# First MLP product of a hybrid decoder block by pairs of column tiles: seven block products in place of eight

## The chip, the cores and the metric

The kernel runs on one core of one Trainium2 chip. The metric is the device time of one execution in microseconds (us), less is better. The core has TensorE (PE in the profile; its weight loads stand apart as PEld), VectorE (DVE), ScalarE (ACT), GpSimd (POOL) and SyncE (SP). The engines run beside each other. Each does its own instructions in the order in which they were written into its queue, and where it needs another engine's result it waits on a semaphore. SyncE's queue issues nearly all the transfers of this kernel.

## The reference, cut to what matters

One layer, 512 positions, width 2048, float32: a mixing sub-layer, then an MLP with a squared ReLU. The change is in the MLP.

```python
# x: (1, 512, 2048); w_ff1: (2048, 8192); w_ff2: (8192, 2048)
x = x + gate1 * (merged @ w_out)
h2 = modulate(rms_norm(x, norm2_g), shift2, scale2)   # rms_norm * (1 + scale2) + shift2
ff = square(relu(h2 @ w_ff1)) @ w_ff2
x = x + gate2 * ff
```

## The kernel before

Everything is held transposed: 128 channels on the partitions, the 512 positions along the free dimension. `h2` is 16 tiles of 128x512 (one for each 128 of the 2048 channels), the hidden layer 64 such tiles, the result `x1` 16.

**Three matmuls for one.** The products are of float32 accuracy from operands of a shorter type (`fp32r`). `split` (L243) makes two tiles of one: ScalarE writes the rounded high part (`hi`), VectorE the remainder (`lo`). `mm3` (L247) issues three matmuls into one PSUM bank: `whi` by `x_hi`, `whi` by `x_lo`, `wlo` by `x_hi`. Each matmul has a weight load of its own.

**Items.** The matmul work is a list of items of 512 weight columns (four weight blocks of 128x128, twelve matmuls). `step` (L334) takes the next one: `pump_loads` issues the transfers of weights for which a buffer `raw` is free (three of 1024 columns), `pump_splits` writes the splits of the items up to two further on into the queues of ScalarE and VectorE (`whi`, `wlo`, four buffers each), then `emit` issues the matmuls and `post` what follows at the end of a tile. So the order on every engine is the order of these calls. A split two items ahead stands in the queue before the work of the present item's `post`.

**Norm stage.** The last tile of the output projection and the first four hidden tiles (`first_emit`, L702) are interleaved by halves of 256 positions with the making of `h2` (`scale_h2`, `shift_h2`, L638 to L650): here, and nowhere else in the products, matmuls stream 256 columns.

**MLP.** The hidden tiles go in eight groups of eight. `add_tile` (L280) of a hidden tile has four items, 48 matmuls. `ff1_post` (L761) applies ReLU and square on ScalarE and splits the result. When a group's eight hidden tiles are there, the second product runs over its share of K: for each of 16 output tiles two items (24 matmuls), then `ff2_post` (L772) adds the product times the gate to `x1[n]` on VectorE. PSUM has eight banks: three of the pool `acc` (every tile's sums) and five of `mx`.

**Memory.** SBUF is one pool `act` with tags: `A` (32 tiles: `h`, later `h2`), `O` (25 tiles: mixing stages, then the hidden tiles), `C`, `T`, `L` and so on.

Of the kernel before, what the change touches and what calls it, by code (L numbers as in the profile page):

```python
# [31 lines left out]
FIRST = ("ident", "adaT")  # L32
SKEW = (1, 3)
# [54 lines left out]
def tile_block(ctx, tc, xT, cT, wada1, wada2, badaT, g1T, g2T, wg0, win, wbat, wbhg, wout, wfg, wff1, wff2,  # L88
               lbT, hggT, qgT, kgT, sinks, table, ident_d, mask_d, onehot_d, neg_d, outT):
# [10 lines left out]
    dram = ctx.enter_context(tc.tile_pool(name="dram", bufs=1, space=bass.MemoryType.DRAM))  # L100

# [59 lines left out]
    def take(tag, shape=None, dt=F32, name=None):  # L161
        pl.live[tag] = pl.live.get(tag, 0) + 1
        return act.tile(shape or [P, T], dt, tag=tag, bufs=BUFS[tag], name=nm(name or tag))

# [51 lines left out]
    ones = fst.tile([P, P], F32, name="ones")  # L216
# [6 lines left out]
    bones = fst.tile([P, P], F32, name="bones")  # L223
# [53 lines left out]
    def add_item(ld, c0, w, emit, pre=None, post=None):  # L277
        items.append((ld, c0, w, emit, pre, post))
# [32 lines left out]
    ahead_of = {}  # L311
    state = {"load": 0, "split": 0, "item": 0}
# [12 lines left out]
    def pump_splits(upto):  # L325
        while state["split"] < min(upto + 1, len(items)):
            ld, c0, w, *_ = items[state["split"]]
            hi = act.tile([P, w], F32R, tag="whi", bufs=BUFS["whi"], name=nm("whi"))
            lo = act.tile([P, w], F32R, tag="wlo", bufs=BUFS["wlo"], name=nm("wlo"))
            split(raws[ld][:, c0:c0 + w], hi, lo)  # L330
            wts[state["split"]] = (hi, lo)
            state["split"] += 1

    def step(ahead=AHEAD, drive=True):  # L334
# [5 lines left out]
        _, _, _, emit, pre, post = items[i]  # L340
# [3 lines left out]
        if post:  # L344
            post()
        if drive:
# [13 lines left out]
    def ada_acc():  # L360
        return act.tile([P, T], F32, tag="aa", bufs=1, name=nm("aa"))

    def ada_rest():
# [4 lines left out]
        def fetch(n):  # L368
            while len(raw) < min(n + BUFS["ada"], 256):
                t = act.tile([P, T], F32, tag="ada", bufs=BUFS["ada"], name=nm("ada"))  # L370
# [213 lines left out]
    def out_post(n):  # L584
        def post(ps):
# [12 lines left out]
            if n == KT - 2:  # L598
                pl.until(lambda: not pl.gens)
                stt(G2, adaT[:, 64:80], 1.0, g2_sb, ALU.add, ALU.mult)  # L600
# [10 lines left out]
    h2 = []  # L611
    kept = []
# [25 lines left out]
    def scale_h2(kt, c=slice(0, T)):  # L638
        if kt == len(h2):
            h2.append((take("A", dt=F32R), take("A", dt=F32R)))  # L640
        t = sqs[kt] = take("T")
        stt(t[:, c], x1[kt][:, c], G2[:, kt:kt + 1], sqs["r"][:, c], ALU.mult, ALU.mult)

    def shift_h2(kt, c=slice(0, T)):
        hi, lo = part(h2[kt], c)
        t = sqs.pop(kt)
# [3 lines left out]
        drop("T")  # L650
# [108 lines left out]
    a_t = {g: [] for g in range(8)}  # L759

    def ff1_post(g):  # L761
        def post(ps):
            r = take("T")
# [622 lines left out]
```

## Time and profile before

| | us |
|---|---|
| median of 3 runs (lowest, highest) | 2766.82 (2766.62, 2767.34) |
| the profiled execution | 2767.79 |
| its span in the trace | 2766.0 |
| TensorE busy in the span | 2743.4 |
| weight loads busy | 2225.9 |
| VectorE busy | 1306.0 |
| ScalarE busy | 932.0 |
| mean granted TensorE clock | 0.999 of 2.4 GHz |

Busy time of TensorE counts overlapping matmuls once, and the ends of matmuls are modelled, so the distance from start to start says more than a duration. The trace gives every instruction with its start, its shape (partitions x columns), and where an engine stood idle the instruction whose end released it. Between span and device time lie 1.8 us, which the change doesn't touch.

### The profile page before, as it was taken

Reading aid. Unit: us, or ns where it says so; the run is one execution under the profiler, and the core shown is the slowest. Engines: PE = TensorE matmul, PEld = TensorE weight load, DVE = VectorE, ACT = ScalarE, POOL = GpSimd, SP = SyncE. Lnnn points to the kernel's source line nnn. Section 1 sums busy time; section 2 is a strip of 40 time slices with the busy share of each in tenths; the row PEclk is TensorE's granted clock in tenths of the full one; section 3 lists DMA queues with packets and bytes.
Section 4 is the critical chain, followed back from the end, with each engine's and each line's share of the span. In section 5 each row is a group of like instructions: output and inputs, shape, how many; then the busy total and the mean of one; then the engine's idle time right before and its main releaser. Section 6 shows DMA issues by size and latency. Waiting matters only on the chain.

```text
span 2766.0 us, 33013 instructions
## 1 busy us (share of the span) xinstructions
PE 2743.4 (99%) x12630; PEld 2225.9 (80%) x12630; DVE 1306.0 (47%) x2574; ACT 932.0 (34%) x1686; POOL 14.5 (1%) x28
## 2 busy tenths in 40 slices
PE   8999999999999999999999999999999999999999
PEld 4777777888888888888888888888888888888887
DVE  4778787655544555565443333332332333323323
ACT  4244455544222322232342332422323223232231
POOL 1000000000000000000000000000000000000000
PEclk9999999999999999999999999999999999999999
DMA  8852322444555555555322222222222322222233
GB/s 322 291 182 93 126 88 73 145 137 138 191 194 191 188 181 184 181 183 186 100 98 101 91 100 99 92 99 99 99 96 96 99 98 93 99 99 92 99 111 111
DMA packets 133790, 369.50 MB, mean 134 GB/s; under 512 B 15168, under 2 KB 15296, under 8 KB 133632
## 3 DMA queue, kind: packets, MB, share of 16 engines
q1 hardware_dynamic: 132480, 364.96, 38.9%
q0 software_dynamic: 1152, 2.43, 0.3%
q8 instruction: 99, 1.62, 0.2%
q14 instruction: 59, 0.48, 0.1%
HBM read 363.11 MB, written 4.23 MB: 133 GB/s over the span
## 4 chain that ended last, share of the span: by engine, by line
PE 97%; DVE 2%; ACT 1%; DMA 0%; issue 0%; SPq 0%; ACTq 0%
PE acc L153 87%; PE mx L153 9%; PE mx L157 1%; DMA C<-xT 0%; DVE wlo L116 0%; ACT T L149 0%; DVE T L120 0%; DVE L L120 0%; DVE T L116 0%; ACT A L149 0%; ACT whi L149 0%; DVE s L1002 0%; DVE C L120 0%; DVE A L120 0%; DVE C L127 0%
## 5 line engine op out<-in xcount | busy, mean ns | idle before, releaser
L153 PE MATMUL acc<-A,whi 128*128 128x512 f32 (+1 forms) x4608 | 1421.7, 390 | 2.4 <-ACT A L149 1.9
L153 PEld LDWEIGHTS acc<-A,whi 128*128 128x128 f32 x4608 | 857.8, 188 | 191.8 <-issue 8.9
L153 PE MATMUL acc<-A,wlo 128*128 128x512 f32 (+1 forms) x2304 | 894.5, 388 | 1.4 <-DVE wlo L116 1.4
L149 ACT ACTIVATE whi<-raw 128x512 fp32r<-128x512 f32 x944 | 569.8, 626 | 918.2 <-PE acc L153 882.6
L116 DVE TENSOR_TENSOR wlo<-raw,whi 128x512 fp32r<-128x512 f32 x944 | 625.9, 686 | 354.9 <-ACT whi L149 354.3
L153 PE MATMUL acc<-O,whi 128*128 128x512 f32 x2560 | 787.9, 389 | 0.0
L153 PEld LDWEIGHTS acc<-O,whi 128*128 128x128 f32 x2560 | 480.5, 188 | 99.7
L153 PEld LDWEIGHTS acc<-A,wlo 128*128 128x128 f32 x2304 | 432.9, 188 | 91.8 <-DVE wlo L116 2.2
L153 PE MATMUL acc<-O,wlo 128*128 128x512 f32 x1280 | 497.9, 389 | 0.0
L120 DVE SCALAR_TENSOR_TENSOR C<-acc,adaT,C 128x512 f32<-128x512 f32 x128 | 96.1, 751 | 432.5 <-PE acc L153 432.5
L153 PEld LDWEIGHTS acc<-O,wlo 128*128 128x128 f32 x1280 | 240.2, 188 | 50.0
L116 DVE TENSOR_TENSOR O<-T,O 128x512 fp32r<-128x512 f32 x64 | 44.4, 693 | 381.7 <-ACT O L149 381.7
L149 ACT ACTIVATE T<-acc 128x512 f32<-128x512 f32 x92 | 55.0, 598 | 460.3 <-PE acc L153 460.3
L387 DVE SCALAR_TENSOR_TENSOR ada<-ada,aa 128x512 f32<-128x512 f32 x256 | 175.6, 687 | 38.3 <-DMA ada<-wada 33.9
L153 PE MATMUL mx<-A,whi 128*128 128x512 f32 (+1 forms) x448 | 134.4, 383 | 3.6 <-ACT A L149 2.5
L153 PEld LDWEIGHTS mx<-A,whi 128*128 128x128 f32 x448 | 81.9, 189 | 25.7 <-issue 5.0
L153 PE MATMUL mx<-A,wlo 128*128 128x512 f32 (+1 forms) x224 | 84.1, 375 | 0.0
L149 ACT ACTIVATE T<-T 128x512 f32<-128x512 f32 (+1 forms) x102 | 62.6, 621 | 6.0 <-DVE T L116 3.4
L149 ACT ACTIVATE T<-C 128x512 f32<-128x512 f32 (+1 forms) x33 | 20.1, 616 | 94.1 <-DVE C L120 90.0
L153 PEld LDWEIGHTS mx<-A,wlo 128*128 128x128 f32 x224 | 42.3, 189 | 8.1
L116 DVE TENSOR_TENSOR O<-mx,O 128x512 f32<-128x512 f32 x56 | 37.9, 688 | 17.1 <-PE mx L153 16.2
L149 ACT ACTIVATE C<-acc 128x512 f32<-128x512 f32 x26 | 15.5, 598 | 86.5 <-PE acc L153 86.5
(155 smaller groups left out, 980.6 us busy)
## 6 DMA issues: line engine op xcount, KB each, us to landing
raw<-wff SPq DMA_DIRECT2D x248, 512.0 KB, 3.3
raw<-win SPq DMA_DIRECT2D x128, 512.0 KB, 3.7
ada<-wada SPq DMA_DIRECT2D x256, 256.0 KB, 4.0
O<-wada SPq DMA_DIRECT2D x128, 256.0 KB, 5.1
raw<-wout SPq DMA_DIRECT2D x32, 512.0 KB, 3.7
raw<-wg SPq DMA_DIRECT2D x24, 512.0 KB, 4.5
raw<-wbat SPq DMA_DIRECT2D x16, 512.0 KB, 3.4
raw<-wbhg SPq DMA_DIRECT2D x16, 512.0 KB, 3.7
```

Source lines behind the costliest of these rows:

```text
L116: nc.vector.tensor_tensor(out=out, in0=in0, in1=in1, op=op)
L120: nc.vector.scalar_tensor_tensor(out=out, in0=in0, scalar=scalar, in1=in1, op0=op0, op1=op1)
L149: nc.scalar.activation(out=out, in_=in_, func=func, **kw)
L153: PE.matmul(out, lhsT=lhsT, rhs=rhs, start=start, stop=stop)
L157: PE.transpose(out=out, in_=in_, identity=ident)
L387: nc.vector.scalar_tensor_tensor(out=t, in0=t, scalar=1.0, in1=cb, op0=ALU.mult, op1=ALU.mult, accum_out=adaq[:, i, q:q + 1])
```

## The change

Two hidden tiles are computed together. The weights of a pair, over two neighbouring channel tiles `e` and `o` of `h2`, are a 2x2 arrangement of 128x128 blocks; `h2` over these two channel tiles and the two halves `a`, `b` of the positions is a 2x2 arrangement of 128x256 blocks. The product of two 2x2 arrangements is done with seven block products instead of eight (Winograd's form of Strassen's scheme): sums of blocks are formed on both sides before, and sums of the products after. Each block product is still three matmuls, now of 256 columns.

- `t_sums`, `t_split`, `t_last` make the four sums of `h2` blocks for each of the eight channel pairs, once, and split them. They overwrite the second half of each even tile of `h2`. `scale_h2` keeps its 16 tiles for it (tag `B`).
- `split_seven` prepares one unit (two channel pairs) of a weight pair: three blocks and four sums of blocks for each, as `hi` and `lo` of 1792 columns (tag `wt`, four buffers, that replaces `whi` and `wlo`).
- `seven_pair` issues four units of 84 matmuls into four banks; `sums1` to `sums3` put the seven products together on VectorE, and ReLU and square follow on ScalarE.
- Hidden tiles 0 to 3 are made as before. Tiles 4 and 5 (`wfp`) are made whole, since the sums are not there yet; tiles 6 to 63 are 29 pairs.
- The second product goes in 16 groups of four hidden tiles (`ff2_group`): 12 matmuls for each output tile, then `ff2_post`.
- A list `todo` holds the sums, the splits of hidden tiles and the `h2` sums; one entry is run at the end of each item. In the last group the first four output tiles take the two hidden tiles that are there first, and the other two after.
- Memory: tags `O` and `L` and the conditioning loads move to a pool `mid` that is closed at the end of the output projection; a pool `mlp` with 32 tiles `B` (sums of `h2`, hidden tiles) takes its place. GpSimd's DMA scratch is set to 1024 bytes.

```diff
-BUFS = {"A": 32, "O": 25, "C": 16, "T": 6, "L": 5, "ada": 3, "raw": 3, "whi": 4, "wlo": 4}
+BUFS = {"A": 32, "O": 25, "C": 16, "T": 6, "L": 5, "ada": 3, "raw": 3, "wt": 4, "B": 32, "S": 1}
+WT = 7 * 2 * P
...
     def pump_splits(upto):
         while state["split"] < min(upto + 1, len(items)):
-            ld, c0, w, *_ = items[state["split"]]
-            hi = act.tile([P, w], F32R, tag="whi", bufs=BUFS["whi"], name=nm("whi"))
-            lo = act.tile([P, w], F32R, tag="wlo", bufs=BUFS["wlo"], name=nm("wlo"))
-            split(raws[ld][:, c0:c0 + w], hi, lo)
-            wts[state["split"]] = (hi, lo)
+            ld, c0, w, *_, prep = items[state["split"]]
+            wts[state["split"]] = prep(raws[ld][:, c0:c0 + w])
...
         if post:
             post()
+        if todo:
+            todo.pop(0)()
...
+    def t_sums(j):
+        a, b = HALF
+        e, o = bare[2 * j], bare[2 * j + 1]
+        sb = adaT[:, 49 + 2 * j:50 + 2 * j]
+        x, y = take("T"), take("T")
+        tt(x[:, a], e[:, b], e[:, a], ALU.subtract)
+        stt(x[:, b], x[:, a], sb, o[:, b], ALU.subtract, ALU.subtract)
+        stt(y[:, a], e[:, b], sd[:, j:j + 1], o[:, b], ALU.add, ALU.subtract)
+        tt(y[:, b], o[:, b], o[:, a], ALU.subtract)
+        tt(y[:, b], y[:, b], x[:, a], ALU.subtract)
...
+    def t_split(j):
...
+        hi, lo = take("B", dt=F32R), take("B", dt=F32R)
+        split(y, hi, lo)
...
+        split(x[:, b], z[:, 0, :], z[:, 1, :])
...
+    def t_last(j):
...
+        hi, lo = part(h2[2 * j], b)
+        split(tb[j][0][:, a], hi, lo)
...
+    def split_seven(raw):
+        hi, lo = wt(), wt()
+        s = take("S", [P, 8 * P])
...
+        tt(v(s[:, 0:2 * c]), v(raw[:, 0:2 * c]), raw[:, 3 * c:4 * c][:, None, :].to_broadcast([P, 2, c]), ALU.add)
+        sact(hi[:, 0:3 * c], raw[:, 0:3 * c], AF.Copy)
+        tt(s[:, 2 * c:3 * c], s[:, 0:c], raw[:, c:2 * c], ALU.add)
+        sact(hi[:, 3 * c:5 * c], s[:, 0:2 * c], AF.Copy)
+        tt(s[:, 3 * c:4 * c], s[:, 2 * c:3 * c], raw[:, 2 * c:3 * c], ALU.add)
+        sact(hi[:, 5 * c:7 * c], s[:, 2 * c:4 * c], AF.Copy)
+        tt(lo[:, 0:3 * c], raw[:, 0:3 * c], hi[:, 0:3 * c].bitcast(F32), ALU.subtract)
+        tt(lo[:, 3 * c:7 * c], s, hi[:, 3 * c:7 * c].bitcast(F32), ALU.subtract)
...
+    def seven_pair(p, now):
...
+                for kp in range(2):
...
+                    for ps, c, w, x in ((b0, a, B11, part(e, a)), (b1, a, B12, part(o, a)), (b1, b, S2, t2),
+                                        (b2, a, S3, t3), (b2, b, S1, t1), (b3, a, B22, t4), (b3, b, S4, part(o, b))):
+                        w += kp * P
+                        mm3(ps[:, c], hi[:, w:w + P], lo[:, w:w + P], x, first and c is a,
+                            last and (c is b or ps is b0))
...
+        def sums1():
...
+            sact(e2[:, 0, :], b0[:, HALF[0]], AF.Copy)
+            tt(e1, b1.rearrange("p (n c) -> p n c", n=2), e2[:, 0:1, :].to_broadcast([P, 2, T // 2]), ALU.add)
...
+        def sums2():
...
+            tt(e2, e1[:, 1:2, :].to_broadcast([P, 2, T // 2]), b2, ALU.subtract)
+            tt(e1[:, 1, :], e2[:, 0, :], b2[:, 1, :], ALU.subtract)
...
+        def sums3():
...
+            tt(e2, e2, b3, ALU.add)
...
+            sact(r0[:, a], e1[:, 0, :], AF.Relu)
+            sact(r0[:, b], e2[:, 1, :], AF.Relu)
+            sact(r0, r0, AF.Square)
...
+            if now:
+                todo.extend([lambda: hidden(r0, g), lambda: hidden(r1, g)])
+            else:
+                waiting.extend([r0, r1])
...
+        for u in range(4):
+            ahead_of[len(items)] = 1 if u < 3 else 2
+            add_item(add_load(wst[p - 3, u], 1024), 0, 1024, unit(u), None, post if u == 3 else None, split_seven)
...
-    for g in range(8):
-        for i in range(8):
-            n = 8 * g + i
-            if n >= GF:
-                add_tile(halves(wff1, n - GF), ready(h2), ff1_post(g))
-        a0 = len(items)
-        for n in range(KT):
-            add_tile([wff2[g, n]], ready(a_t[g]), ff2_post(g, n))
...
+    for i in range(2):
+        add_tile(halves(wfp, i), ready(h2), tiles45(i), (lambda: todo.extend(
+            [shift_diff, lambda: t_sums(0), lambda: t_split(0), lambda: t_sums(1), lambda: t_split(1)])) if i == 1 else None)
+    ff2_group(0)
+    for g in range(1, NG):
+        seven_pair(2 * g + 1, True)
+        if g < NG - 1:
+            seven_pair(2 * g + 2, False)
+        ff2_group(g)
```

What this does to the queues is shown at three places. First TensorE in the middle of the MLP. Before, a hidden tile is one bank (`acc`) with rows of 512 columns:

```order
L153 MATMUL acc_13116<-A_11500,whi_13071 128x512
L153 MATMUL acc_13116<-A_11501,whi_13071 128x512
L153 MATMUL acc_13116<-A_11500,wlo_13072 128x512
L153 MATMUL acc_13116<-A_11536,whi_13071 128x512
L153 MATMUL acc_13116<-A_11537,whi_13071 128x512
L153 MATMUL acc_13116<-A_11536,wlo_13072 128x512
```

After, the first unit of the pair of tiles 10 and 11 (`A`: `h2`, `B`: sums of `h2`, `wt`: weights and their sums):

```order
L163 MATMUL mx_12916<-A_11076,wt_12858 128x256
L163 MATMUL mx_12916<-A_11077,wt_12858 128x256
L163 MATMUL mx_12916<-A_11076,wt_12859 128x256
L163 MATMUL mx_12917<-A_11111,wt_12858 128x256
L163 MATMUL mx_12917<-A_11112,wt_12858 128x256
L163 MATMUL mx_12917<-A_11111,wt_12859 128x256
L163 MATMUL mx_12917<-B_11687,wt_12858 128x256 x2
L163 MATMUL mx_12917<-B_11687,wt_12859 128x256
L163 MATMUL mx_12918<-B_11683,wt_12858 128x256
L163 MATMUL mx_12918<-B_11684,wt_12858 128x256
L163 MATMUL mx_12918<-B_11683,wt_12859 128x256
```

The rows are half as wide, there are seven triples for each channel pair, and they go round four banks.

Second VectorE in the second product of the first group. Before, two remainders of weights and one sum into `x1` for each output tile:

```order
L120 SCALAR_TENSOR_TENSOR C_10393<-acc_12384,adaT,C_10393 128x512
L116 TENSOR_TENSOR wlo_12417<-raw_12329,whi_12416 128x512
L116 TENSOR_TENSOR wlo_12434<-raw_12329,whi_12433 128x512
L120 SCALAR_TENSOR_TENSOR C_10481<-acc_12420,adaT,C_10481 128x512
L116 TENSOR_TENSOR wlo_12453<-raw_12365,whi_12452 128x512
L116 TENSOR_TENSOR wlo_12470<-raw_12365,whi_12469 128x512
L120 SCALAR_TENSOR_TENSOR C_10569<-acc_12456,adaT,C_10569 128x512
```

After, over two output tiles (`sd`: differences of the shifts; `T` to `B`, `T` to `A`: sums of `h2`):

```order
L126 TENSOR_TENSOR wt_11918<-raw_11784,wt_11918 128x512
L130 SCALAR_TENSOR_TENSOR C_10514<-acc_11921,adaT,C_10514 128x512
L126 TENSOR_TENSOR A_11310<-T_11904,A_11309 128x256
L126 TENSOR_TENSOR wt_11937<-raw_11784,wt_11937 128x512
L130 SCALAR_TENSOR_TENSOR C_10598<-acc_11942,adaT,C_10598 128x512
L126 TENSOR_TENSOR T_11956<-B_11355 128x256
L130 SCALAR_TENSOR_TENSOR T_11956<-T_11956,adaT,B_11376 128x256
L130 SCALAR_TENSOR_TENSOR T_11957<-B_11355,sd,B_11376 128x256
L126 TENSOR_TENSOR T_11957<-B_11376 128x256
L126 TENSOR_TENSOR T_11957<-T_11957,T_11956 128x256
L126 TENSOR_TENSOR B_11964<-T_11957,B_11963 128x512
L126 TENSOR_TENSOR B_11967<-T_11956,B_11967 128x256
```

Between the weights' remainders now stand a sum into `x1` for every item and the eight instructions of one channel pair's `h2` sums.

Third TensorE at the end of the last first product. Before, the second product follows with the first of eight hidden tiles, whole:

```order
L153 MATMUL acc_20524<-A_11904,whi_20537 128x512
L153 MATMUL acc_20524<-A_11905,whi_20537 128x512
L153 MATMUL acc_20524<-A_11904,wlo_20538 128x512
L153 MATMUL acc_20600<-O_20060,whi_20555 128x512
L153 MATMUL acc_20600<-O_20061,whi_20555 128x512
L153 MATMUL acc_20600<-O_20060,wlo_20556 128x512
L153 MATMUL acc_20600<-O_20136,whi_20555 128x512
L153 MATMUL acc_20600<-O_20137,whi_20555 128x512
L153 MATMUL acc_20600<-O_20136,wlo_20556 128x512
```

After, behind the last unit of the last pair (`mx_23085`), each output tile begins with two hidden tiles, and goes to the next:

```order
L163 MATMUL mx_23085<-A_11462,wt_23187 128x256
L163 MATMUL mx_23085<-A_11463,wt_23187 128x256
L163 MATMUL mx_23085<-A_11462,wt_23188 128x256
L163 MATMUL acc_23304<-B_23065,wt_23242 128x512
L163 MATMUL acc_23304<-B_23066,wt_23242 128x512
L163 MATMUL acc_23304<-B_23065,wt_23242 128x512
L163 MATMUL acc_23304<-B_23128,wt_23242 128x512
L163 MATMUL acc_23304<-B_23129,wt_23242 128x512
L163 MATMUL acc_23304<-B_23128,wt_23242 128x512
L163 MATMUL acc_23330<-B_23065,wt_23245 128x512
L163 MATMUL acc_23330<-B_23066,wt_23245 128x512
L163 MATMUL acc_23330<-B_23065,wt_23245 128x512
```

The other two hidden tiles of each output tile come after the fourth.

## Rows read from the trace of the kernel before

**Rows 1.** The page's parts 1 and 4: busy time by engine; chain that ended last.

```profile
PE 2743.4 (99%) x12630; PEld 2225.9 (80%) x12630; DVE 1306.0 (47%) x2574; ACT 932.0 (34%) x1686; POOL 14.5 (1%) x28
PE 97%; DVE 2%; ACT 1%; DMA 0%; issue 0%; SPq 0%; ACTq 0%
```

**Rows 2.** Stretches: window; busy us (instructions) by engine; granted clock; DMA share; GB/s.

```profile
1359.14:1362.38 3.24, 3.24 (x29) 3.24 (x28) 2.02 (x5) 1.41 (x4) 0.00 (x0) 1.00 0.00 0
1371.67:1378.50 6.83, 6.83 (x59) 6.83 (x57) 4.48 (x11) 3.08 (x6) 0.00 (x0) 1.00 0.13 53
1413.20:2762.40 1349.20, 1349.13 (x5953) 1116.79 (x5951) 442.69 (x686) 408.85 (x683) 0.00 (x0) 1.00 0.29 98
```

**Rows 3.** Chain of work in order of time, its last long piece: start, us, what.

```profile
1413.22 1349.13 PE acc L153 x5952
```

**Rows 4.** Timeline, TensorE: start, us, operation x count; 256 columns, then 512 columns.

```profile
1373.85 0.40 PE L153 MATMUL mx<-A,whi 128*128 128x256 f32 x2
1374.09 0.28 PE L153 MATMUL mx<-A,wlo 128*128 128x256 f32 x1
1374.21 0.42 PE L153 MATMUL mx<-A,whi 128*128 128x256 f32 x2
1374.48 0.28 PE L153 MATMUL mx<-A,wlo 128*128 128x256 f32 x1
...
2390.89 0.62 PE L153 MATMUL acc<-O,whi 128*128 128x512 f32 x2
2391.57 0.62 PE L153 MATMUL acc<-O,whi 128*128 128x512 f32 x2
```

**Rows 5.** Timeline, weight loads of the same two kinds of stretch.

```profile
1361.06 0.19 PEld L153 LDWEIGHTS acc<-A,wlo 128*128 128x128 f32 x1
1361.18 0.31 PEld L153 LDWEIGHTS acc<-A,whi 128*128 128x128 f32 x2
...
2391.35 0.41 PEld L153 LDWEIGHTS acc<-O,whi 128*128 128x128 f32 x2
2391.80 0.19 PEld L153 LDWEIGHTS acc<-O,wlo 128*128 128x128 f32 x1
```

**Rows 6.** Groups by form, VectorE: busy us, mean ns; idle before, its releaser.

```profile
L116 DVE TENSOR_TENSOR wlo<-raw,whi 128x512 fp32r<-128x512 f32 x944 | 625.9, 686 | 354.9 <-ACT whi L149 354.3
L120 DVE SCALAR_TENSOR_TENSOR C<-acc,adaT,C 128x512 f32<-128x512 f32 x128 | 96.1, 751 | 432.5 <-PE acc L153 432.5
L116 DVE TENSOR_TENSOR T<-acc,T 128x512 f32<-128x512 f32 x16 | 11.1, 692 | 27.9 <-PE acc L153 27.9
L120 DVE SCALAR_TENSOR_TENSOR A<-T,adaT,A 128x256 fp32r<-128x256 f32 x8 | 3.9, 484 | 4.6 <-ACT A L149 4.6
L116 DVE TENSOR_TENSOR C<-C,T 128x256 f32<-128x256 f32 x8 | 3.4, 421 | 0.0
```

**Rows 7.** Groups by form, ScalarE.

```profile
L149 ACT ACTIVATE whi<-raw 128x512 fp32r<-128x512 f32 x944 | 569.8, 626 | 918.2 <-PE acc L153 882.6 <-PE mx L153 29.8 <-issue 4.4
L149 ACT ACTIVATE T<-T 128x256 f32<-128x256 f32 x4 | 1.7, 418 | 0.1
```

**Rows 8.** Timeline, VectorE: two that depend on each other, then the second product.

```profile
1359.67 0.42 DVE L120 SCALAR_TENSOR_TENSOR T<-mx,T 128x256 f32<-128x256 f32 x1 [0.99 <-ACT T L149]
1360.13 0.30 DVE L127 TENSOR_SCALAR T<-T 128x256 f32<-128x256 f32 x1
...
2392.45 0.75 DVE L120 SCALAR_TENSOR_TENSOR C<-acc,adaT,C 128x512 f32<-128x512 f32 x1 [3.49 <-PE acc L153]
2393.12 1.28 DVE L116 TENSOR_TENSOR wlo<-raw,whi 128x512 fp32r<-128x512 f32 x2
```

**Rows 9.** Timeline, TensorE: the longest stop of the norm stage.

```profile
1370.81 0.91 PE L153 MATMUL mx<-A,whi 128*128 128x256 f32 x2 [1.95 <-ACT A L149]
```

**Rows 10.** The page's part 6: weight loads of the MLP, KB each, us to landing.

```profile
raw<-wff SPq DMA_DIRECT2D x248, 512.0 KB, 3.3
```

More of the change, by code (lines that the diff above doesn't have):

```diff
@@ L100, in tile_block, with home @@
     dram = ctx.enter_context(tc.tile_pool(name="dram", bufs=1, space=bass.MemoryType.DRAM))
+    cst.tile([P, FILL], F32, name="fill")
+    late = ctx.enter_context(ExitStack())
+    pools = {"mid": late.enter_context(tc.tile_pool(name="mid", bufs=1))}
+    def home(tag):
+        return pools["mlp"] if tag in MLP else pools["mid"] if tag in MID else act
     uid = [0]
@@ L215, in tile_block @@
     nc.vector.memset(eps, EPS)
-    ones = fst.tile([P, P], F32, name="ones")
+    ones = cst.tile([P, P], F32, name="ones")
     nc.vector.memset(ones, 1.0)
@@ L640, in scale_h2 @@
             h2.append((take("A", dt=F32R), take("A", dt=F32R)))
-        t = sqs[kt] = take("T")
+        if kt not in bare:
+            bare[kt] = take("B")
+        t = bare[kt]
         stt(t[:, c], x1[kt][:, c], G2[:, kt:kt + 1], sqs["r"][:, c], ALU.mult, ALU.mult)
@@ new lines, in ff2_group, with flush, part2, emit @@
+    def ff2_group(g):
+        kept2 = {}
+        def flush():
+            while todo:
+                todo.pop(0)()
+        for n in range(KT):
+            if n % 2 == 0:
+                ld = add_load(wff2[g, n // 2], 1024)
+            early = g == NG - 1 and n < 4
+            def part2(n, ks):
+                hi, lo, ps = kept2[n]
+                for k in ks:
+                    mm3(ps, hi[:, k * P:(k + 1) * P], lo[:, k * P:(k + 1) * P], a_t[g][k], k == 0, k == 3)
+            def emit(hi, lo, n=n, early=early, part2=part2):
+                kept2[n] = (hi, lo, mx() if n < 3 and not early or early and n == 3 else acc())
+                if not early:
+                    pl.until(lambda: len(a_t[g]) == GF)
+                    part2(n, range(4))
+                    return
+                part2(n, range(2))
+                if n == 0:
+                    flush()
+                if n == 3:
+                    for m in range(4):
+                        part2(m, range(2, 4))
+            def post(n=n, early=early):
+                for m in range(4) if early else (n,):
+                    ff2_post(g, m)(kept2.pop(m)[2])
+                    if m == 3 and early or m < 3 and not early:
+                        drop("mx")
+            if early:
+                ahead_of[len(items)] = 3 - n
+            elif n == KT - 1 and g < NG - 1:
+                ahead_of[len(items)] = 1
+            add_item(ld, (n % 2) * T, T, emit, None, post if not early or n == 3 else None)
@@ new lines, in tiles45, with post @@
+    def tiles45(i):
+        def post(ps):
+            waiting.append(relu2(ps))
+            if i == 1:
+                for j in range(KT // 2):
+                    if j > 1:
+                        todo.extend([lambda j=j: (t_sums(j), t_split(j))])
+                    todo.append(lambda j=j: t_last(j))
+        return post
+    for i in range(2):
+        add_tile(halves(wfp, i), ready(h2), tiles45(i), (lambda: todo.extend(
+            [shift_diff, lambda: t_sums(0), lambda: t_split(0), lambda: t_sums(1), lambda: t_split(1)])) if i == 1 else None)
```

132 lines of the change are left out of this document (106 added, 26 removed).

## The prediction

> **What bounds the kernel now.** I read the page's busy times first and the chain of work beside them. TensorE is busy for 2743.4 of 2766.0 us and holds 97% of the chain that ended last; no other engine holds more than 2% of it [rows 1]. So a matmul less is time less, as long as nothing else takes its place. Then I cut out the stretch that the change rewrites, from hidden tile 4 to the last matmul. The chain runs through it in one piece: 5952 matmuls in 1349.13 us [rows 3]. That is 60 hidden tiles x 48 + 8 groups x 16 output tiles x 24 = 2880 + 3072, and 0.22667 us each. The stretches show TensorE busy all of it, VectorE for 443 us and ScalarE for 409 us of 1349, at a granted clock of 1.00, its upper level of 2.4 GHz [rows 2]. There is room beside TensorE for additions, on the average of the stretch; whether there is room at each place has to be asked for each.
>
> The question on which all hangs is what a matmul of 256 columns costs. The norm stage has such matmuls, in the order hi, lo, hi as the new ones. In the timeline three of them start 0.36 us apart from the next three, that is 0.120 us each; three of 512 columns 0.68 us apart, 0.22667 each [rows 4]. The stretch 1359.14 to 1362.38 is 27 starts in 3.24 us without a break, 0.120 [rows 2]. So half the columns cost 0.53, not 0.50: 2 x 0.1200 - 0.2267 = 0.0133 us of each matmul don't depend on its columns.
>
> **The change part by part.**
>
> *Fewer columns.* 58 hidden tiles (6 to 63) x 48 = 2784 matmuls go, 2784 x 0.22667 = 631.0 us. In their place come 29 pairs x 4 units x 84 = 4872 of 256 columns, 4872 x 0.1200 = 584.6 us. That is -46.4 us, and not the eighth of 631 us (79 us) that the count of block products promises. Tiles 4 and 5 and the 3072 matmuls of the second product keep their form. The Trainium skill (TensorE: Matmul & The Clock Gate, Back-to-back issue gap) gives a full-clock spacing of N/2.4 + 2.5 ns; by it 2784 x 0.2158 - 4872 x 0.1092 = 68.8 us would be saved. The rows show a fixed part of 13 ns where that rule has 2.5, and the measurement decides.
>
> *Waits at new weights.* A unit waits for its weights at four matmuls. In the norm stage the start of each twelve, where two new operands are waited for and there already, comes 0.02 us late (0.27 in place of 0.24 inside the three at 1374.21) [rows 4]; at most of the starts before 1362 it costs nothing [rows 2]. For 116 units that is between 0 and 116 x 4 x 0.02 = 9 us. I take one such step a unit, +2 us.
>
> *The `h2` sums.* They fall into the second product of the first group, 16 items of 12 x 0.22667 = 2.72 us, 43.5 us in all. VectorE must get through this before unit 0 of the first pair can start (a remainder of weights 0.69, a sum into `x1` 0.75, 256 columns 0.42 with one tensor operation and 0.48 with the scalar form [rows 6]; two in a row save 0.09 once, 1.28 in place of 1.37, and an operation that needs the one before waits 0.04 more [rows 8]). 14 remainders and 14 sums into `x1`: 14 x 1.44 = 20.2, 17.8 with the savings. Six channel pairs of `t_sums` and `t_split`: 3 x 0.42 + 2 x 0.48 = 2.2, then a wait for ScalarE's high part (0.63 [rows 7], and 0.04), then 0.69 + 0.42: 4.0, or 3.8; six are 22.8 to 24.0. Seven `t_last` 2.5 to 2.9, the split left over of pair 1 1.7, the first part of unit 0's own preparation (0.69 + 0.42 + 0.42, and 0.42 + 256 x 1.04 ns more than a 512 row takes, 0.95, for 768 columns) 2.5. The sum is 47.3 to 51.3 us against 43.5, so TensorE stops for 4 to 8 us in all, some of it piecemeal at the items' weights, the rest at unit 0. I take +7. Below, it could be nearly nothing if VectorE starts with a lead (weights are split two items, 5.4 us, ahead): +2. Above, if every channel pair pays its waits for ScalarE twice: six x 0.7 and more, +13. The nearest row of such a stop is 1.95 us in the norm stage [rows 9].
>
> *The other preparations.* A unit runs 84 x 0.12 = 10.1 us. VectorE needs 0.69 + 0.42 + 0.42 + 0.95 + 1.22 = 3.7 us for it and ScalarE 0.84 + 0.63 + 0.63 = 2.1: hidden between units. The tight place is the first unit of each later group. It is written two items before, so behind the sum into `x1` of the item before: 0.2 us after that item's end (the last three matmuls of a tile start at 2391.57 [rows 4] and take 0.68, the sum starts at 2392.45 [rows 8]), 0.75, then 2.5 us up to what its first matmuls need: ready 3.4 us into a span of 5.44, the rest at 4.6. Hidden, with 0.8 us to spare; cover gone, it costs what is missing, 14 times. The next is item 5 of the second product: ReLU and square of the pair before (six instructions, 2.9 us of ScalarE, behind `sums3`) stand ahead of its weights' cast; ready at about 12.7 us of 13.6. Hidden too. The second sum into `x1` for each output tile (128 more x 0.75 = 96 us of VectorE) lies beside a product that leaves VectorE 1.2 us in each 2.72.
>
> *Banks.* A pair that is finished at once takes the four free `mx` banks, the next one `mx` and three `acc`. Its sums are read by item 2 of the second product; the first `acc` bank is needed at item 3, when `sums1` (behind item 0's sum, about 4.5 us) is long done. Nothing.
>
> *The last group.* Behind the last unit ScalarE first casts two waiting items (1.3 us), VectorE makes their remainders (2.1), then the sums (0.69 + 0.69 + 0.42 + 0.69, to 4.6), ScalarE's ReLU and squares (2.5, to 7.1), cast 0.63 and remainder 0.69: 8.4 us. The four half tiles cover 24 x 0.2267 = 5.4. Left 3.0, less up to 1 for operations in a row. Then the weights of item 4 stand on VectorE behind the fourth sum into `x1`: 0.2 + 0.75 + 0.69 - 0.45 = 1.2. Together +3.5 (1 to 6). Before, the last hidden tile was as late, but seven others of its group covered it.
>
> *Memory and transfers.* Weights are as many bytes; a transfer of 512 KB lands in 3.3 us [rows 10] and is now used for 10 us (units) or 5.4, before for 5.4. The first tiles `B` reuse memory that was last read before the output projection; the stages before tile 4 keep their order. Nothing, with 0 to +2 for a wait that I don't see.
>
> *Sum.* -46.4 + 2 + 7 + 3.5 = -33.9 us. Against the profiled execution's 2767.8 this gives 2733.9; against the median of the runs, 1.0 lower, 2733.
>
> **Rivals.**
>
> *All is hidden.* VectorE has a lead and the waits cost nothing: -46.4 + 3 = -43, 2723. For it, the 443 us of VectorE in 1349; against it, the sum of the first group above.
>
> *Every group stops.* If unit 0 of each later group comes 1 to 2 us late (its spare time is 0.8 us by rows, and the cast of item 5 has 0.9), 14 times, 2733 + 14 to 28 = 2747 to 2761. The same mechanism ends on the other side: at 33.9 / 14 = 2.4 us a group the gain is gone, at 4 us the kernel takes 2733 + 56 = 2789, slower than before. It would need VectorE to be 3 us slower in two items than the rows say, for instance with sums that read three dimensions or PSUM at more than 0.69 us; a row from PSUM has 0.69 [rows 6].
>
> *Weight loads bind.* Each matmul has a load of 0.19 us. With 256 columns loads start 0.12 apart and lie over each other (two in 0.31) [rows 5], and PEld is busy for 3.24 of 3.24 us, at 512 columns for 1117 of 1349 [rows 2]. If in long runs a load had to end before the next, 4872 x (0.188 - 0.120) = +331 us, 3064. Against it, the 57 loads in 6.83 us. The Trainium skill (Perfetto Trace Analysis, Identifying the Most-Contended Engine) judges TensorE's headroom by the busy share of weight loads and not of matmuls; by that rule narrow matmuls leave none. The rows agree that loads are there all the time, and show 0.120 us all the same.
>
> *The fixed part goes.* If the 13 ns hid behind the change of banks, 4872 x 0.0133 = 65 us more, 2668. The three-by-three change of banks is in the norm stage already [rows 4], with the fixed part.
>
> *The change does less than it says.* The old stages could be slowed by the new memory layout; by 33 us it is no change. Their order is the same, so I see nothing that would.
>
> **How the numbers follow.** Forecast 0.70 (2724 to 2746); all hidden 0.08; every group stops 0.16, of which 0.10 still faster, 0.02 no change, 0.04 slower; weight loads 0.01; the fixed part 0.01; old stages slowed 0.04 (0.02 faster, 0.01 no change, 0.01 slower). A measurement of this kernel can tell about 0.2%, 5.5 us, from no change. Faster 0.70 + 0.08 + 0.10 + 0.01 + 0.02 = 0.91, same 0.03, slower 0.06. The range takes in the forecast, half of "all hidden" and the lower part of "every group stops": 2722 to 2750.
>
> **What the profile after would show.** TensorE's matmuls 256 columns wide 0.120 us apart in the units and 168 of them in 20.2 us; weight loads busy nearly all of a unit. Idle time of TensorE before matmuls of the first group's second product and of its first unit, put down to VectorE's or ScalarE's `wt`, of some 7 us; some 3 us in the last group, on `B`; none above 0.3 us elsewhere behind tile 5. The prediction is wrong in its first term if a unit takes other than 10.1 us, and in its others if idle time stands in each group.

## The result and the profile after

| | before | after |
|---|---|---|
| median, us | 2767.08 (2766.62 to 2767.87) | 2733.85 (2732.71 to 2734.99) |
| ratio | | 0.988, 95% interval 0.9863 to 0.9897 |
| profiled execution; its span, us | 2767.8; 2766.0 | 2734.88; 2733.1 |

The forecast was 2733 us, the range 2722 to 2750. The kernel is 33.2 us faster by the medians, 32.9 by the two spans. The profiled execution, from which this kernel's rows below are, is one of the two longer of its four (2734.88 and 2734.99 against 2732.71 and 2732.82 us). Busy time by engine and the chain that ended last, to set beside [rows 1]:

```profile
PE 2704.4 (99%) x14718; PEld 2291.6 (84%) x14718; DVE 1757.9 (64%) x3231; ACT 1042.0 (38%) x1913; POOL 14.6 (1%) x28
PE 96%; DVE 3%; ACT 1%; issue 0%; DMA 0%; SPq 0%; ACTq 0%
```

TensorE still holds the chain, and VectorE has 452 us more to do. The chain in order of time (start, us, what) from the second product of the first group to that of the third:

```profile
1435.96 8.16 PE mx L163 x36
1444.12 2.73 PE acc L163 x12
...
1486.97 21.95 PE mx L163 x169
...
1528.72 8.19 PE mx L163 x36
1536.91 35.36 PE acc L163 x156
1572.27 20.51 PE mx L163 x171
...
1612.59 8.19 PE mx L163 x36
```

A second product begins with the three output tiles in `mx` (8.2 us). From 1528.72 to the next such row is one group: 83.87 us. By spacing it should be 16 x 2.72 + 2 x 20.16 = 83.84. From the first row to 1528.72 it should be 83.84 as well, and is 92.76. So 8.92 us are lost in the first group and 0.03 in the second. Five stops of TensorE in the first, from its timeline (start, us, operation x count, [idle before it, releaser]):

```profile
1464.47 6.13 PE L163 MATMUL acc<-B,wt 128*128 128x512 f32 x24 [0.50 <-ACT wt L159]
1471.09 6.12 PE L163 MATMUL acc<-B,wt 128*128 128x512 f32 x24 [0.49 <-ACT wt L159]
1477.72 6.12 PE L163 MATMUL acc<-B,wt 128*128 128x512 f32 x24 [0.51 <-ACT wt L159]
1484.56 0.50 PE L163 MATMUL mx<-A,wt 128*128 128x256 f32 x2 [0.72 <-ACT wt L159]
1486.97 1.22 PE L163 MATMUL mx<-A,wt 128*128 128x256 f32 x4 [1.91 <-DVE wt L126]
```

Two items (24 matmuls) come every 6.63 us where they need 5.44. The same places by stretches (us, busy us of PE, PEld, DVE, ACT and POOL with their instructions, granted clock, DMA share, GB/s), and two pairs of a later group:

```profile
1435.96:1479.48 43.52, 41.48 (x175) 31.82 (x174) 35.10 (x71) 16.31 (x35) 0.00 (x0) 1.00 0.23 73
1485.00:1488.00 3.00, 1.09 (x6) 1.03 (x6) 2.93 (x6) 2.55 (x5) 0.00 (x0) 0.80 0.13 15
1488.00:1490.00 2.00, 2.00 (x11) 2.00 (x11) 2.00 (x5) 0.28 (x1) 0.00 (x0) 0.50 0.72 246
1572.27:1612.59 40.32, 40.32 (x338) 40.32 (x337) 31.93 (x46) 18.50 (x33) 0.00 (x0) 1.00 0.37 111
```

Behind the last stop the granted clock is 0.50, the lower level of 1.2 GHz; with 0.94 from 1490 to 1492 it costs 3 x 0.20 + 2 x 0.50 + 2 x 0.06 = 1.7 us of the 8.9, the stops the other 7.2. The idle times in the rows come to 4.1 us of these: they count from the modelled ends of matmuls, and behind the stops at 1464.47 and 1471.09 the third weight load waits once more, 0.54 us for VectorE's remainder. The last row shows the narrow matmuls: weight loads are there all the time, and 2 x 168 matmuls take 40.32 us, 0.1200 each. And VectorE has 8.4 us idle in the first row, though TensorE later waits for what it makes: over half of it lies beside items 0 to 4, where TensorE waits for nothing, the rest is 0.70 us in each channel pair, waiting for ScalarE's cast of the sums. In the last group:

```profile
2689.22 0.50 PE L163 MATMUL acc<-B,wt 128*128 128x512 f32 x1 [1.15 <-ACT B L159]
2689.94 4.18 PE L163 MATMUL acc<-B,wt 128*128 128x512 f32 x17 [0.22 <-DVE B L126]
...
2696.93 6.44 PE L163 MATMUL acc<-B,wt 128*128 128x512 f32 x27 [0.99 <-DVE wt L126]
```

The last pair starts at 2662.45; 20.16 + 43.52 us later would be 2726.13, and the last matmul ends at 2729.45: 3.3 us lost. The granted clock stays at 1.00 there. In the groups between, the trace shows no wait of TensorE.

Where the time went, from the end of the norm stage to the last matmul: 1349.13 us before [rows 3], 2729.45 - 1414.20 = 1315.25 after, 33.9 us less. Up to hidden tile 4 the kernel after is 1.0 us later (1414.20 against 1413.22); of that more below.

### The profile page after: what moved, and what is told of

Same layout as the page of the kernel before. It is cut to its first block, busy times and chain, and to the rows that moved or that the text cites. A ratio compares the mean times of both kernels' runs of the same rounds, so it can differ in the third digit from the quotient of the medians.

```text
span 2733.1 us, 38039 instructions
## 1 busy us (share of the span) xinstructions
PE 2704.4 (99%) x14718; PEld 2291.6 (84%) x14718; DVE 1757.9 (64%) x3231; ACT 1042.0 (38%) x1913; POOL 14.6 (1%) x28
## 4 chain that ended last, share of the span: by engine, by line
PE 96%; DVE 3%; ACT 1%; issue 0%; DMA 0%; SPq 0%; ACTq 0%
PE acc L163 68%; PE mx L163 27%; PE mx L167 1%; DVE wt L126 1%; DVE T L126 0%; DVE C L130 0%; DMA C<-xT 0%; ACT T L159 0%; DVE T L130 0%; DVE B L126 0%; DVE L L130 0%; ACT B L159 0%; ACT wt L159 0%; SPq L206 0%; DVE s L1220 0%
## 5 line engine op out<-in xcount | busy, mean ns | idle before, releaser
L163 PE MATMUL acc<-A,wt 128*128 128x512 f32 (+1 forms) x5136 | 1134.6, 369 | 4.1 <-ACT A L159 1.9
L163 PEld LDWEIGHTS acc<-A,wt 128*128 128x128 f32 x5136 | 909.0, 189 | 175.5 <-issue 8.6
L126 DVE TENSOR_TENSOR wt<-raw,wt 128x512 fp32r<-128x512 f32 (+1 forms) x828 | 595.5, 723 | 422.4 <-ACT wt L159 421.4
L159 ACT ACTIVATE wt<-raw 128x512 fp32r<-128x512 f32 (+1 forms) x828 | 530.4, 657 | 835.5 <-PE acc L163 589.8
L163 PE MATMUL acc<-B,wt 128*128 128x512 f32 (+1 forms) x3528 | 734.7, 359 | 4.4 <-ACT wt L159 1.5
L163 PEld LDWEIGHTS acc<-B,wt 128*128 128x128 f32 x3528 | 609.3, 189 | 106.5 <-DVE wt L126 3.6
L163 PE MATMUL mx<-A,wt 128*128 128x256 f32 (+1 forms) x2448 | 428.1, 312 | 4.8 <-ACT A L159 1.9
L163 PEld LDWEIGHTS mx<-A,wt 128*128 128x128 f32 x2448 | 362.6, 193 | 36.2 <-issue 5.0
L163 PE MATMUL mx<-B,wt 128*128 128x256 f32 (+1 forms) x1632 | 297.7, 320 | 0.0
L163 PEld LDWEIGHTS mx<-B,wt 128*128 128x128 f32 x1632 | 250.5, 191 | 20.7
```

What stands on the lines that cost most here:

```text
L126: nc.vector.tensor_tensor(out=out, in0=in0, in1=in1, op=op)
L159: nc.scalar.activation(out=out, in_=in_, func=func, **kw)
L163: PE.matmul(out, lhsT=lhsT, rhs=rhs, start=start, stop=stop)
```

## The experiments

The early stages reach hidden tile 4 at 1411.4 to 1414.2 us, in no order that the edits would explain. Losses below are therefore taken between rows of the chain: in the first group from the start of its second product, less 83.84 us, and in the last group from the start of its last pair, less 63.68 us. The kernel after loses 8.9 and 3.3 us by these.

**The price of narrow matmuls.** In the kernel before, hidden tiles 6 to 34 with 256 columns, 35 to 63 with 128:

```diff
                     for k in range(4):
-                        mm3(cell["ps"], hi[...], lo[...], x[k0 + k], ...)
+                        for s in range(parts):
+                            c = slice(s * T // parts, (s + 1) * T // parts)
+                            mm3(cell["ps"][:, c], hi[...], lo[...], (x[k0 + k][0][:, c], x[k0 + k][1][:, c]), ...)
...
-                add_tile(halves(wff1, n - GF), ready(h2), ff1_post(g))
+                add_tile(halves(wff1, n - GF), ready(h2), ff1_post(g), None, 1 if n < 6 else 2 if n < 35 else 4)
```

> The kernel before with narrower matmuls in its first MLP product and nothing else changed: hidden tiles 6 to 34 use 256 columns (96 matmuls a tile in place of 48), hidden tiles 35 to 63 use 128 columns (192 a tile). A tile of 512 columns takes 48 x 0.22667 = 10.88 us. Theory, a fixed part of 0.0133 us for each matmul and nothing more: 256 columns 0.120 us apart, a tile 11.52 us; 128 columns 0.0667 us apart, a tile 12.80 us; in all 29 x 0.64 + 29 x 1.92 = 18.6 + 55.7 = +74 us, about 2841 us. Rival, the weight loads set a floor near the 0.12 us at which they were seen apart: 256 columns as above, but 128 columns stay 0.12 us apart, a tile 23.0 us; 18.6 + 29 x 12.16 = +371 us, about 3138 us. Second rival, the fixed part is larger where the moving operand is a slice of a wider tile: 256 columns more than 0.122 us apart.

Measured: 3093.7 us, between the two. One tile of each kind, and the last piece of the chain:

```profile
1738.58:1750.10 11.52, 11.52 (x98) 11.52 (x97) 3.19 (x5) 4.05 (x8) 0.00 (x0) 1.00 0.30 92
2701.56:2723.00 21.44, 21.44 (x195) 21.44 (x193) 3.28 (x6) 4.17 (x8) 0.00 (x0) 1.00 0.16 50
...
1414.00 1674.23 PE acc L153 x11520
```

At 256 columns a tile takes 11.52 us = 96 x 0.1200, as the fixed part of 0.0133 us says; so the second rival, a dearer slice, falls. At 128 columns it takes 21.44 us = 192 x 0.1117, not 192 x 0.0667. The whole piece agrees: 1674.23 less 3168 x 0.22667 and 2784 x 0.1200 leaves 622 us for 5568 matmuls, 0.1117 each. Both theories miss: there is a floor, but a little under the 0.12 that the rival took. No other engine is waited for in that stretch, so something that each of these matmuls brings of its own sets it. Its weight load doesn't shrink with the columns, which makes it the likely part; no run here separates it from other costs of one matmul. 256 columns stand 7% above this floor, 128 lie on it. The Trainium skill (Perfetto Trace Analysis, Identifying the Most-Contended Engine) judges TensorE by the busy share of its weight loads. Here that share is full in both rows, and the time is free of the floor in the first and bound by it in the second: the share warns, and only the spacing decides.

**No sums of `h2`.** Six of the eight channel pairs take the sums of another:

```diff
                     if j > 1:
-                        todo.extend([lambda j=j: (t_sums(j), t_split(j))])
-                    todo.append(lambda j=j: t_last(j))
+                        todo.append(lambda j=j: (drop("B", 2), tb.update({j: list(tb[1])})))
+                    else:
+                        todo.append(lambda j=j: t_last(j))
```

> The kernel after, but the sums of h2 are formed for channel pairs 0 and 1 alone; the other six channel pairs reuse those of pair 1, so six of the eight preparations are left out and the output is not the reference's. Theory (VectorE's sums in the second product of the first group stop TensorE there, and the stop of some 2 us then lets the clock fall): all 8.9 us lost in that group go, the clock stays at 1.00 behind it, about 2725 us. Rival, unit 0's own preparation behind the weights and sums of items 13 to 15 is what stops TensorE: the stops before items 10 to 14 (1.5 us) go, and 7 us of the loss stay, about 2732 us.

Measured: 2723.85 us (2723.00 to 2724.38).

```profile
1433.98 8.16 PE mx L163 x36
...
1517.82 8.19 PE mx L163 x36
```

83.84 us, nothing lost, and the granted clock is 1.00 behind the second product. All 8.9 us come from the sums; unit 0's own preparation stops nothing when they are gone.

**Sums on GpSimd.** Five of a pair's operations go there from channel pair 2 on, for instance

```diff
-        tt(y[:, b], o[:, b], o[:, a], ALU.subtract)
+        G.tensor_tensor(out=y[:, b], in0=o[:, b], in1=o[:, a], op=ALU.subtract)
```

> The kernel after, with five of the operations of each of the channel pairs 2 to 7's sums of h2 (three subtractions and two remainders) moved from VectorE to GpSimd, which is otherwise idle there; nothing else is changed but the order in which these steps are written. Theory (VectorE is overfull in the second product of the first group): VectorE has about 10 us less to do there, and 6 to 8 us of the 8.9 us lost come back, about 2726 to 2728 us. Rival, the chain through ScalarE and the items' order, not VectorE's load, sets the stop: no gain, 2733 to 2735 us. Second rival, GpSimd takes so long for a 256-column row (over 2 us) that the sums come later than now, or VectorE's own operations beside it grow by over a fifth: slower, 2738 us or more.

Measured: 2732.36 us (2732.14 to 2733.76). The first group loses 8.0 us (1433.96 to 1525.79), so 0.9 come back and not 6 to 8; by the times alone the kernel can't be told from the kernel after. VectorE and GpSimd side by side, then VectorE and ScalarE one channel pair later:

```profile
1469.22 0.74 DVE L130 SCALAR_TENSOR_TENSOR C<-acc,adaT,C 128x512 f32<-128x512 f32 x1
1469.88 1.26 DVE L126 TENSOR_TENSOR B<-T,B 128x512 fp32r<-128x512 f32 x1
1471.06 1.22 DVE L126 TENSOR_TENSOR wt<-raw,wt 128x512 fp32r<-128x512 f32 x1
...
1469.86 1.88 POOL L809 TENSOR_TENSOR T<-B 128x256 f32<-128x256 f32 x2
1471.81 1.06 POOL L809 TENSOR_TENSOR T<-T,T 128x256 f32<-128x256 f32 x1
...
1475.32 0.80 DVE L126 TENSOR_TENSOR wt<-raw,wt 128x512 fp32r<-128x512 f32 x1 [1.58 <-ACT wt L159]
...
1473.83 0.94 ACT L159 ACTIVATE B<-T 128x512 fp32r<-128x512 f32 x2 [4.54 <-DVE T L130]
1474.67 0.61 ACT L159 ACTIVATE wt<-raw 128x512 fp32r<-128x512 f32 x1
```

A remainder beside a busy GpSimd takes 1.22 to 1.26 us in place of 0.69 [rows 6]; the sum into `x1`, which reads one operand from PSUM, keeps its 0.74. The Trainium skill (SBUF, State Buffer; SBUF: two separate sides) says that these engines lock a shared port pair against each other when VectorE reads two operands from SBUF, and the rows agree. The slower remainders took back part of what VectorE gave away and not all: in the first 46.04 us of the second product it is busy for 34.0 us, in the kernel after for 37.6. But in each channel pair it now stands idle for 1.58 us until ScalarE has cast the next weights, behind the cast of the sums. So a pair takes 6.8 us, more than the 6.63 of the kernel after, and the 0.9 us come back at unit 0, whose stops add up to 1.5 us in place of 2.6. The first rival, that the chain through ScalarE and the items' order sets the stop and not VectorE's load alone (2733 to 2735 us), is nearer than the theory, and the next run takes it up.

**The same work in another order.** In the kernel after, VectorE waits for ScalarE between a pair's sums and their remainders, and ScalarE's casts of the next weights stand behind the casts of the sums. After's rows (VectorE, then ScalarE):

```profile
1469.12 0.42 DVE L126 TENSOR_TENSOR T<-T,T 128x256 f32<-128x256 f32 x1
1470.25 1.03 DVE L126 TENSOR_TENSOR B<-T,B 128x512 fp32r<-128x512 f32 x2 [0.70 <-ACT B L159]
1471.19 0.68 DVE L126 TENSOR_TENSOR wt<-raw,wt 128x512 fp32r<-128x512 f32 x1
...
1469.58 0.94 ACT L159 ACTIVATE B<-T 128x512 fp32r<-128x512 f32 x2 [4.34 <-DVE T L126]
1470.43 0.61 ACT L159 ACTIVATE wt<-raw 128x512 fp32r<-128x512 f32 x1
```

ScalarE sat idle for 4.34 us and still casts the weights late, since the cast of the sums is ahead in its queue. The edit puts casts and remainders one item later, behind that item's weights:

```diff
                     if j > 1:
-                        todo.extend([lambda j=j: (t_sums(j), t_split(j))])
-                    todo.append(lambda j=j: t_last(j))
+                        todo.append(lambda j=j: t_sums(j))
+                        todo.append(lambda j=j: (t_cast(j), t_rest(j)))
```

> The kernel after; for channel pairs 2 to 7 the sums of h2 are formed in one item of the second product, and their high parts are cast and their remainders formed in the next item, behind that item's own weights. The same operations on the same engines, in another order. Theory (in each of these pairs VectorE stands idle 0.70 us for ScalarE's cast of the sums, and ScalarE's casts of the next weights stand behind that cast): without the wait, 6 x 0.70 = 4.2 us come back, the stops before items 10, 12 and 14 go, and 2729 to 2730 us are left. Rival (VectorE has 5.9 us of work for each two items of 5.44 us, and that alone sets the stop): 0.5 x 6 = 3 us of the 8.9 us stay and the stops move towards unit 0, at most 1 us is gained, 2732 to 2734 us.

Measured: 2727.85 us (2727.39 to 2728.69).

```profile
1434.72 8.16 PE mx L163 x36
...
1522.53 8.19 PE mx L163 x36
```

87.81 us, 4.0 lost: 4.9 are back, and the stops before items 10, 12 and 14 are gone. Of the 4.0, 1.8 are waits for unit 0's weights, and the clock is at 0.50 behind them from 1482 to 1484. So the order between VectorE and ScalarE was over half of the loss. The edit undoes two things at once, VectorE's wait and the weights' late cast behind it; six waits of 0.70 us come to 4.2 of the 4.9, but the run doesn't separate the two. VectorE, no longer idle from 1445.64 to unit 0, now needs 5.84 us for a channel pair and its two items, against 5.44 for the items: it is overfull there, as the theory of the GpSimd run said, and that and the clock behind the stop leave the 4.0. The next run moves part of this work to where there is room.

**Begun earlier.** With the order of the run above, and pairs 0 to 3 beside hidden tiles 4 and 5, pairs 4 to 7 one in three items:

```diff
         add_tile(halves(wfp, i), ready(h2), tiles45(i), (lambda: todo.extend(
-            [shift_diff, lambda: t_sums(0), lambda: t_split(0), lambda: t_sums(1), lambda: t_split(1)])) if i == 1 else None)
+            [shift_diff] + [f for j in range(4) for f in (
+                lambda j=j: t_sums(j), lambda j=j: (t_cast(j), t_rest(j)))])) if i == 0 else None)
```

> The kernel after with the sums of h2 apart as in e6_apart, and begun two hidden tiles earlier: those of channel pairs 0 to 3 beside hidden tiles 4 and 5, those of pairs 4 to 7 beside the second product, one pair in three items. The same operations on the same engines. Theory (VectorE's work in the first group has room, 9 us idle beside hidden tiles 4 and 5 and 5.8 us beside items 0 to 4, but stands too late in the program): all 8.9 us come back, the clock stays at 1.00 behind the second product, about 2725 us. Rival: the tail of the norm stage needs VectorE beside hidden tile 4, so the sums delay the evictions or the weights there, and 2 to 5 us are lost again: 2727 to 2730 us.

Measured: 2724.01 us (2723.76 to 2724.77). TensorE waits for nothing from hidden tile 4 to the last group:

```profile
1433.90 8.16 PE mx L163 x36
...
1517.74 8.19 PE mx L163 x36
```

83.84 us, nothing lost, with every operation still on its engine. The sums fit; they stood in the wrong places.

**The last group without half tiles.**

```diff
-            early = g == NG - 1 and n < 4
+            early = False
```

(and the waiting steps are run before item 0).

> The kernel after, with the last group in the plain order: no half tiles ahead of its second product, which starts with item 0. Theory of the prediction: behind the last unit VectorE and ScalarE need about 8.4 us until the first weights and the squares of the last pair are there, the half tiles cover 5.4 us of it; without them the whole chain lies open, so the stop there grows from 3.4 us to 7 to 8.5 us, +4 to +5 us, about 2738 us. Rival, the waits in the last group are those for item 4's weights behind the four sums into x1 and not the chain behind the last unit: then the half tiles cover little, 2733 to 2735 us.

Measured: 2737.54 us (2737.24 to 2739.74). The last pair starts at 2662.43, the chain's last row ends at 2698.93 + 35.37 = 2734.30: 8.2 us lost in place of 3.3, +4.9 as expected in the profiled execution (2739.74 us), +3.7 by the medians. TensorE's longest stop, the wait for the cast of the last pair's squares:

```profile
2688.66 10.28 PE L163 MATMUL mx<-B,wt 128*128 128x512 f32 x30 [4.69 <-ACT B L159]
```

4.7 us of the loss are this stop. The rest lies behind it: the granted clock is 0.50 from the restart to 2695, and the last 186 matmuls take 3.5 us more than 186 x 0.22667.

**The last group in another order on VectorE.**

```diff
                 if n == 0:
+                    for _ in range(2):
+                        todo.pop(0)()
+                    while owed:
+                        owed.pop(0)()
                     flush()
...
+                    if early:
+                        pump_splits(state["item"] + m)
```

(`owed` holds the remainders of items 2 and 3; the first two steps are `sums2` and `sums3`).

> The kernel after with two steps of the last group in another order: the sums of the last pair stand ahead of the remainders of items 2 and 3's weights on VectorE, and the weights of items 4 to 7 are each prepared behind one of the four sums into x1 and not behind all four. Theory (both stops in the last group, 1.4 and 1.0 us, are queue order on VectorE): under 0.7 us of the 3.4 us stay, about 2731 us. Rival: the first stop is the chain through ScalarE (five ReLUs and squares, two casts, 3.5 us) whatever VectorE does first; then only the second stop goes, 2732.5 to 2733 us, not to be told from the kernel after.

Measured: 2730.92 us (2729.05 to 2731.73).

```profile
2662.17 20.15 PE mx L163 x168
...
2693.23 32.65 PE acc L163 x144
```

The last matmul ends 63.71 us behind the pair's start, so 0.03 us are lost and 3.3 are back. The rival falls: the chain through ScalarE, from the ReLUs to the last cast, is as long as before (3.4 us) and now starts early enough.

**Both together.**

> e7_early and e8_last together: if the two stretches are independent the gains add up, 8.9 + 2.7 to 3.4 us, 2721 to 2723 us. Rival: what is gained in the first group comes back as a wait in a later one, or the early sums cost something in the norm stage: 2725 us or more.

Measured: 2721.23 us (2719.86 to 2722.57), ratio to the kernel before 0.9833 (0.9818 to 0.9848), 12.6 us under the kernel after by the medians. No wait of TensorE is left in either stretch. From hidden tile 4 (1411.36) to the last matmul (2714.39) it takes 1303.0 us, 46.1 less than before: the first term of the sum, bare.

**How much a later group can bear.** In group g, g additions that nothing reads stand ahead of the next group's unit 0:

```diff
+                if n == 13 and 0 < g < NG - 1:
+                    t = take("T")
+                    for _ in range(g):
+                        tt(t, x1[n], x1[n], ALU.add)
+                    drop("T")
```

> The kernel after with extra work on VectorE that nothing reads: in group g (1 to 14) g additions of 128x512 stand behind the sum into x1 of item 13, right ahead of the preparation of the next group's unit 0. An addition in a row costs 0.60 us, so the delays grow from 0.6 to 8.4 us in one execution. Theory of the prediction (unit 0 of a later group has 0.8 us to spare): groups from 2 on stop TensorE by 0.6 g - 0.7 us, in all some 53 us, about 2787 us. Rival, read from the trace of after: unit 0's remainders end 1.9 to 2.3 us before their matmuls and unit 1's 0.9 us before theirs, with 0.5 us of idle VectorE between them, so 1.4 us are to spare and unit 1 is the tight place: no stop in groups 1 and 2, some 0.4 us in group 3, then 0.6 us more in each, in all some 44 us, about 2778 us. The granted clock behind each stop is read as well: if it falls at a length of its own, the stops above that length show it and those below don't.

Measured: 2799.9 us. The starts of the second products of groups 1 to 7 (the chain):

```profile
1526.77 8.19 PE mx L163 x36
...
1610.63 8.19 PE mx L163 x36
...
1694.60 8.19 PE mx L163 x36
...
1779.27 8.19 PE mx L163 x36
...
1864.67 8.19 PE mx L163 x36
...
1950.79 8.19 PE mx L163 x36
...
2038.36 8.19 PE mx L163 x36
```

Less 83.84, groups 1 to 6 lose 0.02, 0.13, 0.83, 1.56, 2.28 and 3.73 us. From group 3 on each addition adds 0.72 to 0.73, which is its true pitch (three of them 2.15 us in VectorE's timeline; 0.60 was taken). 3 x 0.72 - 0.83, 4 x 0.72 - 1.56 and 5 x 0.72 - 2.28 all give 1.3 us to spare. So the first theory falls, the rival's 1.4 us is near, and both totals miss: this pitch and 1.3 us to spare take the rival's 44 us to some 58, and group 6 shows the rest. It jumps by 1.45, because behind its stop the clock fell, and not behind group 5's (timeline, then stretches):

```profile
1909.64 0.73 PE L163 MATMUL mx<-A,wt 128*128 128x256 f32 x4 [1.20 <-DVE wt L126]
...
1996.49 1.02 PE L163 MATMUL mx<-A,wt 128*128 128x256 f32 x4 [1.92 <-DVE wt L126]
...
1911.00:1913.00 2.00, 2.00 (x18) 2.00 (x18) 2.00 (x4) 0.00 (x0) 0.00 (x0) 1.00 0.60 229
1997.00:1999.00 2.00, 2.00 (x11) 2.00 (x11) 2.00 (x4) 0.48 (x1) 0.00 (x0) 0.50 0.75 217
```

It fell in every longer one too, up to 7.7 us, and cost 0.6 to 1.8 us each time whatever the stop's length (a group's loss less 0.72 g - 1.3; groups 6 to 13).

## Why the prediction was right, step by step

*Fewer columns: right.* -46.4 was predicted, and the kernel with both orders changed, without the losses in the first and last group, shows -46.1, the waits at new weights among it. The fixed part of 0.0133 us is there at 256 columns and explains why seven block products in place of eight save 46 and not 79 us. So the rivals by which it goes, or by which weight loads bind at this width, are refuted.

*A slip in the working.* The count "29 pairs x 4 units x 84" is 9744, not 4872. A unit has 42 matmuls and a pair 168, as the row at 1572.27 shows with two pairs in 40.32 us; "four units of 84" in the description of the kernel and "a unit runs 10.1 us" are wrong by two, and so is the sign by which the first term was to be judged. The total of 4872 and its price were right. The slip fell on *the other preparations*: VectorE needs some 3.5 us for a unit, and 4.1 from unit 0's first addition to unit 1's, between which a hidden tile's remainder stands (1573.58 and 1577.70 in its timeline), out of 5.04 and not out of 10.1. It is still hidden, but the tightest room inside a pair is 0.9 us and not 6. A unit's transfer likewise has 5 us and not 10; TensorE waits for none.

*Waits at new weights: too high.* +2 was taken; the thirteen groups from 1528.72 to 2618.90 take 83.86 us each, so a group loses 0.02 us, some 0.3 in all, the lower end.

*The `h2` sums: right in place and near in size, incomplete in mechanism.* +7 with a range of 2 to 13, measured 8.9. The sum of VectorE's work, 47.3 to 51.3 us against 43.5, contains 0.7 us of waiting for ScalarE in each pair. In the trace a pair and its two items take 6.63 us, 5.93 of work and these 0.70, against 5.44; with that order undone 4.9 of the 8.9 come back. What the step did not have is that ScalarE's weight casts queue behind the waiting cast, and the 1.7 us at half clock behind the stop. The lead that would have hidden all was on VectorE, 9 and 5.8 us idle beside hidden tiles 4 and 5 and beside items 0 to 4; the program as written didn't use it.

*Later groups: right, the tight place wrong.* No group stops. The spare time is 1.3 us where 0.8 was worked out, so the rival "every group stops" is refuted with its price: the measured slope past the spare time is one for one, as that rival assumed.

*The last group: right in kind, the size in part luck.* +3.5 predicted, 3.3 measured, and both stops stand where they were expected. But the chain behind the last unit, worked out at 8.4 us, takes 6.8 (2682.44 to 2689.22), and 6.2 in the run without half tiles (2682.42 to 2688.66). The three idle times in the rows come to 2.4 us, and the other 0.9 lies at the matmuls around them, whose ends are modelled. That the run without half tiles loses 8.2 us in all does not confirm the 8.4, since some 3 of these are the clock.

*Old stages: +1.0 in the profiled execution, where nothing was predicted.* 0.3 us is there before 677 us (677.13 against 676.85), but other kernels with the same early stages reach that point at 675.0 to 677.6, so no cause is to be read from it. The other 0.7 goes with the clock in the norm stage. The stop of [rows 9] is there again, and behind it the clock is 1.00 before [rows 2] and 0.50 after:

```profile
1371.09 9.15 PE L163 MATMUL mx<-A,wt 128*128 128x256 f32 x49 [1.94 <-ACT A L159]
...
1372.00:1374.00 2.00, 2.00 (x11) 2.00 (x11) 0.90 (x3) 1.00 (x2) 0.00 (x0) 0.50 0.47 188
```

*The sum.* -46.1, with the waits at new weights in it, + 8.9 + 3.3 = -33.9, as measured between hidden tile 4 and the end; -33.9 had been predicted. Terms that were off by -1.7 (waits), +1.9 (sums) and -0.2 us (last group) cancelled, so the agreement of the stretch to 0.1 us is luck, and the agreement to some 2 us in each term is not.

## What to carry to other kernels

Price a smaller matmul by its spacing at that very width: the saved columns came with a fixed part at 256, and with a floor at 128 where another halving would have lost. When work moves to an engine that is idle on average, ask where it stands in that engine's queue and in the queue of whoever feeds it: the same operations, cast one item later and begun two tiles earlier, cost 8.9 us or nothing. A stop of TensorE cost its length here and, where the clock fell behind it, 0.6 to 3 us more.

## What was not expected of the hardware

- Behind most stops of some 2 us and more the granted clock was 0.50 for some 3 to 7 us, worth 0.6 to 1.8 us, and some 3 us behind the 4.69 us of the last group without half tiles. No length decides it alone: behind the same stop of 1.94 to 1.96 us in the norm stage it fell in four of the profiles (among them the kernel after and the narrow one) and stayed at 1.00 in the others, the kernel before among them; it fell behind 1.92 us and longer in the ramp and not behind 1.20; it fell behind 1.61 and 0.16 us in the run with the same work in another order, and not behind 1.15, 0.22 and 0.99 us in the last group of the kernel after; and it fell behind two stops of 0.65 and 0.66 us in close succession in the run with GpSimd. What else it hangs on stays open.
- A matmul that loads 128x128 weights of its own came 0.1117 us behind the one before, on the mean of 5568, at 128 columns and a clock of 1.00.
- An addition that reads one tile twice and writes the tile of the addition before it took 0.72 us in a row, where remainders in a row take 0.60.
